# One encoder layer on one core: w_down's squares moved into the joint MLP, and five smaller changes of order, banks and queues

## The chip, the cores and the metric

The kernel runs on one core of a Trainium2 chip as one launch. The metric is device time in microseconds (us), from the start of the program to its end. The engines are TensorE (PE), VectorE (DVE), ScalarE (ACT), GpSimd (POOL) and SyncE (SP). SP, ACT and POOL also issue DMA transfers, each in its own order; all transfers of the core run on the same 16 DMA engines.

## The reference

One layer of an encoder on 2048 tokens of width 1024, in float32, cut here to what is computed:

```python
y = rmsnorm(h, norm_mix_g) @ w_in                    # q, k, v (8 heads of 64) and the conv's a, g
att = dilated_sliding_attention(q, k, v)             # three patterns (window, stride), joined by their lse
conv = silu(layernorm(depthwise_conv31(a * sigmoid(g))))
h = h + concat(att, conv) @ w_out
xq = rmsnorm(h, norm_x_g) @ w_xq                     # 4 heads of 256 against 256 memory tokens
h = h + softmax(xq @ xk.T) @ xv @ w_xo               # xk, xv = rmsnorm(mem) @ w_xk, w_xv
u = rmsnorm(h, norm_mlp_g) @ w_up                    # 1024 -> 4096
h = h + square(relu(u)) @ w_down                     # 4096 -> 1024
out = rmsnorm(h, norm_final_g)
```

## The kernel before, in words

**Arithmetic.** A float32 operand is split into a high part (a cast, mostly on ACT) and a low part (operand minus high part, mostly on DVE), and a product is three matmuls: high by high, low by high, high by low (`mm3`, L270 to L272). So every weight block of 128x1024 is loaded, cast (`whi_…`), subtracted (`wlo_…`) and then used by PE. Where the parts are float16, the weights are first scaled by a power of two that comes from the sum of the weight's squares (`pow2_scale`), so that the low parts do not vanish.

**Stages.** The 2048 tokens are four quarters p = 0 to 3 of 512.

1. 0 to about 390 us: `w_in`. The norm and transposes of x for each quarter (`xprep`: `xn`, `xv`, `xh`, `xl`), the products `lin` with the weight blocks `g0` … `a3` of the conv (`lwhi_g20` is the high part of block g2's weights, L226), q, k, v, RoPE. A generator `steps` walks PE's products; others are woven into it. `later` is the x work of quarters 2 and 3, `qks` the squares of the q and k weights (ACT L781, loads on SP). ACT's Sigmoid (`sig`, L672) empties the PSUM bank of a `lin`.
2. About 390 to 690 us: attention of quarter 0, with the memory's products beside it (class `Matrices`). `load(i)` fetches weight block i (0 to 15 w_xk and w_xv, 16 to 23 w_xq, 24 to 31 w_xo) on POOL's queue, into a ring of two buffers `raw` that w_out's blocks `raw_o…` use next, or, for 26 to 29, into buffers of their own in the pool `back_w`, which opens when the attention's pool closes. `turn` transposes w_xq (PE writes bank `xqt`, ACT copies the high part, DVE subtracts the low part, L539 to L542), `score` multiplies it by the memory's keys, `back` multiplies w_xo by the memory's values (`pb`) and stores the result (`eb` to `bscr`) on POOL's queue. `ps(tag, …)` takes a PSUM bank: "mm" has two, "T" two more, which the attention's transposes use.
3. About 690 to 1310 us, `post(0)`, and to 1860 us, `post(1)`: w_out (`o`), cross attention (`xs`, `x`) and the MLP (`up`, `dn`) of a quarter, with the attention of the next quarter beside it. In `post(0)` each MLP block's low part is stored to DRAM (`lou`, `lod`), and `post(1)` loads it back. In `post(1)` ACT also squares every block of w_up and w_down, 32 each, and sums the squares (`wsq`, L1571), for the scales of stage 5.
4. To about 2145 us: `before_mlp(2)` and `(3)`, the same without the MLP.
5. From about 2137 us: the MLP of quarters 2 and 3 together, as a 2x2 block product with seven products in place of eight (Strassen's scheme: `b11`, `b21`, `t1` … are sums of quarters of the operands). In the first half, 7 early products (`PRO`, weights `whi_ua0` … `whi_ua6`, result `r11_…`) precede 16 calls of `up_pair`; DVE forms sums of the bank's results (`r`), ACT applies Relu (L1812) and Square (L1813, which also sums), and POOL's queue stores the result (`keep_r`, `rb`, `rt`). In the second half four sweeps p, q, r, s over the 16 pairs multiply by w_down; each step loads a hidden block and its weights, scales and splits them (`bh`, `bl`, `whi`, `wlo`, L1798 and L1799) and runs 12 matmuls for each of its one or two products. Between the sweeps DVE adds the seven products into the result: `plus` (L1986, SBUF with SBUF) and `join` (L1989, with a bank).

Each engine runs its instructions in the order that a scheduler fixed when the program was built; `after(…)`, `pinned` and `weave` only steer that order. An attention pattern's result `o1` goes to DRAM (`oscr`) and is loaded again by `combine` (`ld`), since it has another token order.

## Time and profile before

| | |
|---|---|
| median of 3 runs | 2778.16 us (2777.91 to 2783.6) |
| the profiled execution | 2774.07 us, span 2772.3 us |
| PE busy | 2661.1 us of the span, 96% |
| DVE, ACT, POOL busy | 1918.8, 1359.5, 589.4 us |
| DMA | 535.68 MB, mean 193 GB/s |

The profile is of one execution. Its own time stands 1.8 us above its span, and 4.1 us below the median. PE's 14,787 matmuls are pipelined, so a busy PE is not one at its peak: in some stretches its clock is granted only half, and a matmul of 512 columns then starts every 0.43 us instead of every 0.216 us. Such stretches count as busy; the column PEclk of the windows shows them.

### The profile page before, as it was taken

To read this page: it belongs to the slowest core of one execution; us is meant where nothing else is said; L and a number is where in the kernel's file an instruction comes from. 1 tells how busy PE (TensorE), PEld (TensorE's weight loads), DVE (VectorE), ACT (ScalarE), POOL (GpSimd) and SP (SyncE) were. 2 spreads that over 40 slices of the span, in tenths; PEclk is the share of its full clock that TensorE was granted. 3 is DMA by queue.
4 is the path that set the end of the run, shared out by engine and by line. 5 is a ranking of instruction groups with operands and counts; after the bars stand their busy time and mean duration, and the time that the engine had idled before them with its cause. 6 is when DMAs were issued, how large, how long until landed. Compare 5 with 4: busy or idle time off the path is not lost.

```text
span 2772.3 us, 40744 instructions
## 1 busy us (share of the span) xinstructions
PE 2661.1 (96%) x14787; PEld 1831.0 (66%) x14787; DVE 1918.8 (69%) x3508; ACT 1359.5 (49%) x2354; POOL 589.4 (21%) x807
## 2 busy tenths in 40 slices
PE   7899999988999999999999999999999999989998
PEld 4444457876777878788777777877887444434444
DVE  4568726665788876578976477756475887767776
ACT  6742217655454333434455555564343545545445
POOL 6474313543102212200111201121010122200000
PEclk9999999999999999999999999999999999999999
DMA  7874457887636666766457766764633564485553
GB/s 252 217 200 113 135 182 200 244 238 229 200 114 204 203 220 208 246 215 208 133 177 225 240 210 201 238 226 158 190 114 126 178 205 167 168 304 170 171 189 110
DMA packets 459816, 535.68 MB, mean 193 GB/s; under 512 B 98172, under 2 KB 329200, under 8 KB 459616
## 3 DMA queue, kind: packets, MB, share of 16 engines
q1 hardware_dynamic: 420992, 406.52, 48.5%
q0 software_dynamic: 36752, 123.06, 12.7%
q10 hardware_dynamic: 1872, 3.52, 0.3%
q8 instruction: 116, 1.90, 0.3%
q14 instruction: 84, 0.69, 0.1%
HBM read 384.46 MB, written 148.52 MB: 192 GB/s over the span
## 4 chain that ended last, share of the span: by engine, by line
PE 60%; DMA 13%; issue 11%; ACT 5%; DVE 5%; POOL 4%; SPq 2%; POOLq 0%; ACTq 0%; DVEq 0%
PE dn L270 4%; PE dn L271 4%; PE dn L272 4%; PE up L270 3%; PE up L272 3%; PE up L271 3%; PE lin L270 2%; PE lin L272 2%; PE lin L271 2%; SPq L57 2%; PE x L270 2%; PE x L271 2%; PE x L272 2%; PE xs L270 2%; PE xs L272 2%
## 5 line engine op out<-in xcount | busy, mean ns | idle before, releaser
L287 DVE SCALAR_TENSOR_TENSOR cacc<-cu,cwu,cacc 128x512 f32<-128x512 f32 x480 | 395.6, 826 | 6.8
L1032 ACT ACTIVATE sm<-sm,o 128x256 f32<-128x256 f32 (+1 forms) x384 | 159.2, 466 | 115.3 <-DVE o L1031 114.8
L270 PE MATMUL dn<-hhh,whi_d 128*128 128x512 f32 x512 | 202.1, 405 | 5.8 <-ACT hhh L1591 3.5
L270 PE MATMUL up<-mh,whi_u 128*128 128x512 f32 x512 | 203.9, 399 | 1.7 <-ACT whi_u L1567 1.7
L271 PE MATMUL dn<-hhl,whi_d 128*128 128x512 f32 x512 | 200.6, 394 | 0.8 <-DVE hhl L1592 0.8
L272 PE MATMUL up<-mh,wlo_u 128*128 128x512 f32 x512 | 200.0, 391 | 0.0
L272 PE MATMUL dn<-hhh,wlo_d 128*128 128x512 f32 x512 | 199.9, 393 | 0.0
L271 PE MATMUL up<-ml,whi_u 128*128 128x512 f32 x512 | 199.6, 390 | 0.0
L1042 DVE TENSOR_TENSOR pl<-pt,ph 128x512 f16<-128x512 f32 x160 | 109.6, 685 | 80.3 <-ACT ph L1041 79.8
L1031 DVE CUSTOM_DVE_ANT_0 sm<-s,mask 128x256 f32<-128x256 f32 (+1 forms) x384 | 126.6, 373 | 33.5 <-DMA oscr<-o 11.8
L1041 ACT CAST ph<-pt 128x512 f16<-128x512 f32 x160 | 92.2, 576 | 77.0 <-PE pt L1038 76.3
L1606 DVE TENSOR_TENSOR h<-h,dn 128x512 f32<-128x512 f32 x128 | 85.9, 682 | 55.6 <-PE dn L272 55.0
L247 POOL TENSOR_TENSOR nr<-st_v,mhalf 128x4 f32<-128x4 f32 x12 | 13.2, 1098 | 513.2 <-DVE st_v L243 513.2
L270 PEld LDWEIGHTS dn<-hhh,whi_d 128*128 128x128 f32 x512 | 95.5, 188 | 25.8 <-ACT hhh L1591 5.2
L272 PEld LDWEIGHTS dn<-hhh,wlo_d 128*128 128x128 f32 x512 | 96.6, 189 | 20.3
L270 PEld LDWEIGHTS up<-mh,whi_u 128*128 128x128 f32 x512 | 96.2, 188 | 20.6 <-ACT whi_u L1567 2.0
L271 PEld LDWEIGHTS dn<-hhl,whi_d 128*128 128x128 f32 x512 | 96.7, 189 | 19.6 <-DVE hhl L1592 1.8
L272 PEld LDWEIGHTS up<-mh,wlo_u 128*128 128x128 f32 x512 | 96.1, 188 | 20.5
L271 PEld LDWEIGHTS up<-ml,whi_u 128*128 128x128 f32 x512 | 96.3, 188 | 18.6
L270 PE MATMUL o<-cath,whi_o 128*128 128x512 f32 x256 | 103.0, 403 | 4.3 <-ACT whi_o L261 3.6
L272 PE MATMUL o<-cath,wlo_o 128*128 128x512 f32 x256 | 101.5, 398 | 1.4 <-DVE wlo_o L262 1.4
L1038 PE MATMUL pt<-ident,sm 128*128 128x128 f32 x640 | 100.1, 274 | 2.7 <-ACT sm L1032 2.5
(647 smaller groups left out, 7835.8 us busy)
## 6 DMA issues: line engine op xcount, KB each, us to landing
raw_u<-in_w_up_dram SPq DMA_DIRECT2D x64, 512.0 KB
raw_d<-in_w_down_dram SPq DMA_DIRECT2D x64, 512.0 KB
k<-kscr SPq DMA_DIRECT2D x32, 640.0 KB
raw_a<-ascr SPq DMA_DIRECT2D x32, 512.0 KB
raw_b<-bscr SPq DMA_DIRECT2D x32, 512.0 KB
lou<-wlo_u POOLq DMA_DIRECT2D x32, 512.0 KB, 5.4
lod<-wlo_d POOLq DMA_DIRECT2D x32, 512.0 KB, 5.5
wlo_u<-lou SPq DMA_DIRECT2D x32, 512.0 KB
```

Source lines behind the costliest of these rows:

```text
L57: return (q or nc.sync).dma_start(o, i)
L247: last["pow"] = POOL.tensor_tensor(dst, v, mhalf.to_broadcast([P, v.shape[1]]), op=ALU.pow)
L270: PE.matmul(o, lh, rh, start=first, stop=False)
L271: PE.matmul(o, lh, rl, start=False, stop=False)
L272: last["pe"] = PE.matmul(o, ll, rh, start=False, stop=end)
L287: DVE.scalar_tensor_tensor(acc, u[:, t:t + 512], cwu[:, c, t:t + 1], acc, op0=ALU.mult, op1=ALU.add)
L1031: last["dve"] = DVE.tensor_tensor_reduce(dst, so, mask[:, 256 * m:256 * m + nk], 1.0, 3e38, ALU.add, ALU.min, mn)
L1032: last["act"] = ACT.activation(dst, dst, AF.Exp, bias=mn, scale=-1.0)
L1038: last["pe"] = PE.transpose(pt[:, j, :], sm[:, j, :], ident)
L1041: ACT.copy(ph, pt)
L1042: DVE.tensor_tensor(pl, pt, ph, op=ALU.subtract)
L1606: last["dve"] = DVE.tensor_tensor(hs[m], hs[m], pt, op=ALU.add)
```

## The change

Seven edits, in the order of the program.

**(a)** `last["g2"]` is set where `steps` reaches the cast of block g2, and `later` and `qks` may be placed only behind it.

**(b)** `turn`'s second transpose bank (g = 1) comes from "T" instead of "mm": four banks in turn instead of two.

**(c)** Blocks 26 and 27 of w_xo now use the ring `raw`, and 28 to 31 the buffers of `back_w`; 26 and 27 are loaded as soon as the ring is free, and `raw_o00` and `raw_o01` find it free earlier.

**(d)** 13 stores `oscr<-o1` move from ACT's queue to POOL's.

**(e)** In `post(1)` the squares of w_down go; those of w_up stay.

**(f)** In the first half of stage 5 a new generator `down_squares` loads w_down once more, 32 loads of 512 KB on POOL's queue into two buffers in turn, and ACT squares each in place with a sum. Three steps of it follow each of the first two pairs, and two each of the next. Then a sum over the 32 columns, one small matmul and `pow2_scale` give the scale that the sweeps use. Some small columns change their tile (`cw` and `wscl` swap roles).

**(g)** 4 of DVE's `plus` go from behind sweep q into sweep q, and 12 from ahead of sweep r's joins and sweep s into sweep r, one per step from the third step on.

```diff
@@ class Matrices
-            if 25 < i < 30:
+            if i > 27:
                 raw = self.bl.tile([P, 2, 512], F32, tag=f"rb{i}", name=f"raw_m{i}")
...
-                    pt = ps("mm", f"xqt{i}{g}")
+                    pt = ps("T" if g else "mm", f"xqt{i}{g}")
...
-            if i < 26:
-                self.load(i + 6)
...
                 if mc == 0:
                     self.split(i + 1)
+                    if i == 24:
+                        self.load(27)
@@ w_in
         drain(islice(steps, 10))
+        last["g2"] = last["split"]
...
-        later = pinned(chain(xprep(sp, 2), islice(mem, 1), xprep(sp, 3), mem), "x1_7", "flo", "pe")
-        qks = pinned(qkscale(), "x1_7", "xs1")
+        later = pinned(chain(xprep(sp, 2), islice(mem, 1), xprep(sp, 3), mem), "x1_7", "g2", "flo", "pe")
+        qks = pinned(qkscale(), "x1_7", "g2", "xs1")
@@ attention
-                    os_.rearrange("p b h e -> p b (h e)"), None if far and pr < 3 else nc.scalar)
+                    os_.rearrange("p b h e -> p b (h e)"), None if far and pr < 3 else nc.gpsimd)
...
             mats.split(24)
+            mats.load(26)
...
-            for i in range(26, 30):
+            for i in range(28, 32):
                 mats.load(i)
@@ def wmlp (post(1))
-        j = tmp("wsq").bitcast(BF16).rearrange("p (a b) -> p a b", a=shape[1])
-        x = i + (DFF // P if w == "d" else 0)
-        ACT.activation(j, raw, AF.Square, accum_out=fw[:, x:x + 1])
+        if w == "u":
+            j = tmp("wsq").bitcast(BF16).rearrange("p (a b) -> p a b", a=shape[1])
+            ACT.activation(j, raw, AF.Square, accum_out=fu[:, i:i + 1])
@@ joint MLP, first half
+    def down_squares():
+        sq = [pm.tile([P, D], F32, tag="dsq", name=f"dsq{k}", bufs=2) for k in range(2)]
+        for k in range(DFF // P):
+            if k > 1:
+                sq[k % 2] = pm.tile([P, D], F32, tag="dsq", name=f"dsq{k}", bufs=2)
+            dma(sq[k % 2], w_down[P * k:P * k + P], nc.gpsimd)
+            yield
+            if k:
+                t = sq[(k - 1) % 2]
+                ACT.activation(t, t, AF.Square, accum_out=wscl[:, k - 1:k])
...
+        DVE.tensor_reduce(v[:, 0:1], wscl, axis=AX.X, op=ALU.add)
+        norm_scale("d", c30, v, mc[:, 1:2], mc[:, 3:4])
+        yield
...
     for i in range(NP):
         prev = up_pair(i, early_pairs[i] if i < PRO else None, prev)
+        drain(islice(down, 3 if i < 2 else 2))
+    drain(down)
     prev()
@@ sweeps
-    def sweep(tag, blocks, weights, kinds):
+    def sweep(tag, blocks, weights, kinds, side=iter(())):
...
+            if k > 1:
+                next(side, None)
+        drain(side)
...
-    m4, m6 = sweep("q", ("t4", "t2"), w_second, "XY")
+    m4, m6 = sweep("q", ("t4", "t2"), w_second, "XY", adds([(HD_[2][m], e1[m]) for m in range(4)]))
     for m in range(4):
-        plus(HD_[2][m], e1[m], DVE)
...
-    m2, m5 = sweep("r", ("b21", "t1"), w_third, "XY")
+    m2, m5 = sweep("r", ("b21", "t1"), w_third, "XY",
+                   adds([x for m in range(4) for x in ((HD_[2][4 + m], e7[m]), (HD_[3][4 + m], e7[m]),
+                                                       (HD_[3][m], e1[m]))]))
...
-    for m in range(4):
-        plus(HD_[2][4 + m], e7[m], DVE)
-        plus(HD_[3][4 + m], e7[m], DVE)
-        plus(HD_[3][m], e1[m], DVE)
```

What this moves in the fixed orders is shown at three places. First ACT near 66 us of the span, before the change. `xn2`, `xn3` are x's rows of quarters 2 and 3, `qks` loaded weights of q and k, `sig0_1` the Sigmoid that empties the bank in which PE's next product starts:

```order
L381 ACTIVATE junk_940,ssx2_933<-xn2_1_1_916 128x512
L781 ACTIVATE qks00_960,qka_959<-qks00_960 128x512
L381 ACTIVATE junk_942,ssx2_933<-xn2_2_0_919 128x512
L781 ACTIVATE qks01_963,qka_959<-qks01_963 128x512
L381 ACTIVATE junk_944,ssx2_933<-xn2_2_1_920 128x512
L381 ACTIVATE junk_946,ssx2_933<-xn2_3_0_923 128x512
L381 ACTIVATE junk_948,ssx2_933<-xn2_3_1_924 128x512
L381 ACTIVATE junk_1276,ssx3_1275<-xn3_0_0_1211 128x512
L226 CAST lwhi_g20_693<-lraw_g20_679 128x1024
L672 ACTIVATE sig0_1_988<-lin_899,wscl_328 128x512
```

The same place on ACT with the change:

```order
L419 CAST xh3_1_416<-xv1_7_866 128x512
L226 CAST lwhi_g20_693<-lraw_g20_679 128x1024
L381 ACTIVATE junk_934,ssx2_933<-xn2_0_0_911 128x512
L781 ACTIVATE qks00_960,qka_959<-qks00_960 128x512
L781 ACTIVATE qks01_963,qka_959<-qks01_963 128x512
L672 ACTIVATE sig0_1_988<-lin_899,wscl_328 128x512
```

The cast of g2's weights now leads, and one x square and two q/k squares stand ahead of the Sigmoid instead of eleven such squares, of which eight are shown, and the cast.

Second, POOL's queue near 660 us, before the change (`eb` are results of `back` on their way to `bscr`; `raw_m30` and `raw_m31` were issued some 20 rows earlier, and `raw_o00` follows seven `bscr` stores later):

```order
L57 DMA bscr_111<-eb000_7811 128x4x128
L57 DMA bscr_111<-eb010_7821 128x4x128
L57 DMA raw_m26_7772<-in_w_xo_dram 128x2x512
L57 DMA raw_m27_7774<-in_w_xo_dram 128x2x512
L57 DMA raw_m28_7776<-in_w_xo_dram 128x2x512
L57 DMA raw_m29_7778<-in_w_xo_dram 128x2x512
L57 DMA bscr_111<-eb001_7847 128x4x128
L57 DMA bscr_111<-eb011_7857 128x4x128
```

The same place on POOL with the change (`raw_m26` and `raw_m27` have taken the earlier places of 30 and 31):

```order
L57 DMA bscr_111<-eb000_7813 128x4x128
L57 DMA bscr_111<-eb010_7823 128x4x128
L57 DMA raw_m28_7774<-in_w_xo_dram 128x2x512
L57 DMA raw_m29_7776<-in_w_xo_dram 128x2x512
L57 DMA raw_m30_7778<-in_w_xo_dram 128x2x512
L57 DMA raw_m31_7780<-in_w_xo_dram 128x2x512
L57 DMA raw_o00_8093<-in_w_out_dram 128x8x128
L57 DMA bscr_111<-eb001_7847 128x4x128
L57 DMA bscr_111<-eb011_7857 128x4x128
L57 DMA raw_o01_8099<-in_w_out_dram 128x8x128
```

The four loads at this place are now of blocks that PE needs two blocks later, and w_out's first two loads stand here.

Third, ACT near 2146 us, in the early products, before the change (`r11_0` from `b1_0` is the Relu that empties the bank in which PE's next early product starts, the second `r11_0` its Square, `whi_ua5` the next weights, `Y…` casts of operands):

```order
L1812 ACTIVATE r11_0_22181<-b1_0_22153,wscl_328 128x512
L1826 COPY c1_1_22204<-b1_1_22191 128x512
L1547 COPY rsb3_20571<-nrb_21997 128x512
L1813 ACTIVATE r11_0_22181,cw_322<-r11_0_22181 128x512
L1724 CAST Yb22h0_22025<-yn3_01_22037 128x512
L1724 CAST Yt1h0_22048<-yt1_0_22042 128x512
L1724 CAST Yt2h0_22009<-yt2_0_22043 128x512
L1724 CAST Yt3h0_22017<-yt3_0_22052 128x512
L1798 ACTIVATE whi_ua5_22339<-raw_ua5_22337,wscl_328 128x1024
L1812 ACTIVATE r11_1_22219<-b1_1_22191,wscl_328 128x512
```

The same place on ACT with the change:

```order
L1817 ACTIVATE r11_0_22117<-b1_0_22089,cw_322 128x512
L1831 COPY c1_1_22140<-b1_1_22127 128x512
L1549 COPY rsb3_20507<-nrb_21933 128x512
L1907 ACTIVATE dsq1_22441,wscl_328<-dsq1_22441 128x1024
L1818 ACTIVATE r11_0_22117,cw_322<-r11_0_22117 128x512
L1729 CAST Yb22h0_21961<-yn3_01_21973 128x512
L1729 CAST Yt1h0_21984<-yt1_0_21978 128x512
L1729 CAST Yt2h0_21945<-yt2_0_21979 128x512
L1907 ACTIVATE dsq2_22445,wscl_328<-dsq2_22445 128x1024
L1729 CAST Yt3h0_21953<-yt3_0_21988 128x512
L1803 ACTIVATE whi_ua5_22275<-raw_ua5_22273,cw_322 128x1024
L1817 ACTIVATE r11_1_22155<-b1_1_22127,cw_322 128x512
```

Two squares of w_down stand between one Relu and the next, and the second waits for a load that may start only when the square two before it is done. On ACT, 16 of the 32 squares stand ahead of the last early Relu, `r11_6`, and all 32 ahead of `r4_2`, the first result of the fifth pair.

More of the change, by code (lines that the diff above doesn't have):

```diff
@@ L1662, in hybrid_layer, with norm_scale @@
     late = ExitStack()
+    def norm_scale(x, c30, v, c, inv):
+        pc = ps("c", f"fwp{x}")
+        with ExitStack() as st:
+            after(st, "pe")
+            PE.matmul(pc[:, 0:1], c30, v[:, 0:1], start=True, stop=True)
+        DVE.tensor_scalar(v[:, 2:3], pc[:, 0:1], 1e-30, None, op0=ALU.max)
+        pow2_scale(c, inv, v[:, 2:3], v[:, 4:5], -1)
     def mlp_scales():
@@ L1668, in mlp_scales @@
         DVE.memset(c30, 2.0 ** -30)
-        DVE.tensor_reduce(v[:, 0:2], fw.rearrange("p (x k) -> p x k", x=2), axis=AX.X, op=ALU.add)
+        DVE.tensor_reduce(v[:, 0:1], fu, axis=AX.X, op=ALU.add)
         g8 = gv[:, GV["mlp"]:GV["mlp"] + 8]
@@ L1673, in mlp_scales @@
         yield
[L1674 to L1679 removed]
+        norm_scale("u", c30, v, mc[:, 0:1], mc[:, 2:3])
         yield
@@ L1690, in mlp_scales @@
         yield
-    mc, gml = wscl[:, 0:16], wscl[:, 16:24]
+    mc, gml = spare[:, 96:112], spare[:, 112:120]
     scales = mlp_scales()
@@ L1891, in up_pair @@
         return rest
+    def down_squares():
[8 more added lines that the diff above has]
+                ACT.activation(t, t, AF.Square, accum_out=wscl[:, k - 1:k])
+        t = sq[(DFF // P - 1) % 2]
+        ACT.activation(t, t, AF.Square, accum_out=wscl[:, 31:32])
+        yield
+        v = spare[:, 64:80]
+        c30 = pm.tile([P, P], F32, name="c30d")
+        DVE.memset(c30, 2.0 ** -30)
+        DVE.tensor_reduce(v[:, 0:1], wscl, axis=AX.X, op=ALU.add)
+        norm_scale("d", c30, v, mc[:, 1:2], mc[:, 3:4])
+        yield
+    down = down_squares()
     early_pairs = [True] * PRO
@@ L1998, in hybrid_layer, with adds @@
             dma(HD_[p][k], hscr[p, k])
-    m4, m6 = sweep("q", ("t4", "t2"), w_second, "XY")
+    def adds(items):
+        for a, b in items:
+            plus(a, b, DVE)
+            yield
+    m4, m6 = sweep("q", ("t4", "t2"), w_second, "XY", adds([(HD_[2][m], e1[m]) for m in range(4)]))
     for m in range(4):
-        plus(HD_[2][m], e1[m], DVE)
         join(HD_[2][4 + m], m4[m], HD_[2][4 + m])
```

8 lines of the change are left out of this document (1 added, 7 removed).

## The prediction

> **What bounds the kernel now.** First the page's list of engines, then PE's waits.
>
> ```profile
> PE 2661.1 (96%) x14787; PEld 1831.0 (66%) x14787; DVE 1918.8 (69%) x3508; ACT 1359.5 (49%) x2354; POOL 589.4 (21%) x807
> ```
>
> PE is the bound: it idles 2772.3 - 2661.1 = 111 us. No edit takes matmuls away (one tiny one is added), so only this idle time and the time at half clock can be won. PE's waits, as total, times and longest:
>
> ```profile
> PE r L271 <- DVE bl_r L1799: 6.9, 3, 3.8
> ...
> PE xqt L539 <- DVE wlo_m L542: 6.1, 5, 1.8
> PE lin L270 <- ACT sig L672: 6.1, 1, 6.1
> ...
> PE b L1791 <- ACT r L1812: 5.2, 4, 1.6
> ...
> PE pb L270 <- ACT whi_m L261: 3.9, 1, 3.9
> ...
> PE o L270 <- ACT whi_o L261: 3.6, 2, 3.3
> ...
> PE dn L270 <- ACT hhh L1591: 3.5, 6, 1.1
> ...
> PE dn L270 <- ACT whi_d L1567: 2.3, 3, 1.3
> ...
> PE pb L271 <- DVE wlo_m L262: 0.8, 1, 0.8
> ```
>
> Each of these but `b` is aimed at by one edit; `b` is the one that (f) may lengthen. A wait costs more than itself where the clock drops behind it, which the windows show (PE busy is the first column, the clock the number behind the counts, then DMA share and GB/s):
>
> ```profile
> 70.00:78.00 8.00, 1.89 (x12) 1.16 (x11) 2.49 (x9) 6.52 (x17) 1.83 (x2) 0.81 0.46 163
> 78.00:85.00 7.00, 6.36 (x17) 2.51 (x16) 4.11 (x9) 7.00 (x18) 3.28 (x3) 0.50 0.90 268
> 664.00:672.00 8.00, 3.37 (x10) 2.43 (x9) 3.17 (x4) 2.74 (x4) 2.16 (x3) 0.80 0.96 305
> 690.00:700.00 10.00, 6.36 (x17) 4.04 (x16) 6.67 (x21) 2.48 (x4) 2.21 (x3) 0.66 1.03 360
> 1714.00:1726.00 12.00, 10.30 (x53) 7.20 (x52) 6.98 (x11) 10.44 (x19) 0.00 (x0) 0.86 0.60 187
> 2140.00:2180.00 40.00, 34.22 (x162) 15.70 (x160) 33.69 (x54) 26.24 (x48) 7.15 (x12) 1.00 0.42 135
> 2627.00:2647.00 20.00, 14.40 (x59) 6.04 (x58) 20.00 (x29) 9.52 (x14) 0.00 (x0) 0.91 0.50 150
> ```
>
> Half of what PE works at half clock is lost. From 78 to 85 us that is 6.36 / 2, with a little before it 3.5 us. A mean of 0.80 over 8 us is 3.2 us at half clock, nearly all worked, so 1.5 us lost; 0.66 over 10 us is 6.8, so 3.2; 0.86 over 12 us is 3.4, so 1.6; 0.91 over 20 us is 3.6, so 1.7.
>
> **The change part by part.**
>
> (a) The cast of g2. ACT around it now:
>
> ```profile
> 71.38 0.63 ACT L781 ACTIVATE qks<-qks 128x512 f32<-128x512 f32 x1 [5.49 <-DMA qks<-in_w_in_dram]
> ...
> 76.11 1.03 ACT L226 CAST lwhi_g<-lraw_g 128x1024 f16<-128x1024 f32 x1
> 77.04 0.68 ACT L672 ACTIVATE sig<-lin,wscl 128x512 f32<-128x512 f32 x1
> ```
>
> PE waits for the Sigmoid. In the new order two q/k squares still stand ahead of it, and the first has its data only at 71.4, so the Sigmoid ends near 71.4 + 2 x 0.8 + 0.7 = 73.7: 4.1 of the 6.1 us go. A wait of 2 us is no longer than those of `xqt`, so the 3.5 us of clock go too, by my estimate. But the next weights, g3, are now cast behind two more q/k squares, whose loads SP issues only after others at a DMA share of 0.9, while PE comes 4 us earlier: I take 3 us back. Gain 5, between 0 and 9.6.
>
> (b) Four banks. With two more, a transpose waits for the subtraction four groups back, not two. The attention uses these banks as well, so I take 4 of 6.1, between 0 and 6.1.
>
> (c) w_xo and w_out. From 640 to 720 us, KB each and median to landing:
>
> ```profile
> raw_o<-in_w_out_dram POOLq DMA_DIRECT2D x6, 512.0 KB, 7.0
> raw_m<-in_w_xo_dram POOLq DMA_DIRECT2D x4, 512.0 KB, 7.2
> ```
>
> Blocks 26 and 27 are now loaded before the attention's buffers come free, so 3.9 + 0.8 and 1.5 of clock go. Block 28 inherits the late place, but PE needs it some 7 us after block 26 (24 matmuls of 0.23 us and some of the attention's), against the 3.9 by which block 26 came late: I leave 1 us, since the four loads at this place slow one another, gain 5. Block o00 is asked for ahead of seven stores: 3.3 us of wait and 3.2 of clock may go; but 690 to 700 us has a DMA share of 1.03, the same bytes must arrive, and PE comes 6 us earlier. The stores that the two loads pass are read only in `post(0)`. I take 4. Gain 9 in all, between 3 and 6.2 + 3.6 + 3.2 = 13.
>
> (d) The stores on POOL. ACT loses 13 issues; POOL's in-order queue gains them, and `oscr3_1` now sits behind the `bscr` store of `eb111`. The combine that reads it ends on DVE, and PE transposes its result:
>
> ```profile
> 697.44 1.41 DVE L1170 TENSOR_TENSOR cat<-cat,ld 128x512 f32<-128x512 f32 x2
> ...
> 709.89 0.60 PE L1178 MATMUL catT<-ident,cat 128*128 128x128 f32 x4
> ```
>
> That leaves 11 us of slack, which (c) shortens by about 4. 0, between -2 and +2.
>
> (e) No squares of w_down in `post(1)`.
>
> ```profile
> L1571 ACT ACTIVATE wsq<-raw_d 128x1024 bf16<-128x1024 f32 x32 | 33.6, 1049 | 0.0
> ```
>
> ACT gives up 33.6 us, but it was not the bound; the worth is PE's waits for it: 3.5 for `hhh` (queued behind a square), 2.3 for `whi_d` (its load starts when the square has let the buffer go), 1.6 of clock. What is late next is the DMA of the same blocks. 5, between 2 and 7.4.
>
> (g) The sums. DVE between sweeps q and r:
>
> ```profile
> 2629.43 1.89 DVE L1986 TENSOR_TENSOR hd<-hd,e 128x512 f32<-128x512 f32 x3
> 2631.24 1.27 DVE L1799 SCALAR_TENSOR_TENSOR bl_r<-braw_r,wscl,bh_r 128x1024 f16<-128x1024 f32 x1
> 2632.43 5.50 DVE L1986 TENSOR_TENSOR hd<-hd,e 128x512 f32<-128x512 f32 x9
> ...
> 2640.38 1.27 DVE L1799 SCALAR_TENSOR_TENSOR bl_r<-braw_r,wscl,bh_r 128x1024 f16<-128x1024 f32 x1
> 2641.58 0.74 DVE L1799 SCALAR_TENSOR_TENSOR wlo_r<-raw_dd,wscl,whi_r 128x512 f16<-128x512 f32 x1
> ...
> 2646.62 0.68 DVE L1982 TENSOR_TENSOR keep<-raw_dd,keep 128x512 f32<-128x512 f32 x1
> ```
>
> Twelve sums of 0.61 us stood ahead of the `bl_r` that PE waited for (6.9 us, and 1.7 of clock). One a step, they fit: a step costs DVE two `wlo_r`, one `bl_r` and two of the last kind, 4.1 us, and PE works 24 x 0.216 = 5.2. The joins stay, so I take 5 of 8.6, at least 2.
>
> (f) The squares in the joint MLP: the one cost. ACT in the early products now:
>
> ```profile
> 2146.54 0.67 ACT L1812 ACTIVATE r<-b,wscl 128x512 f32<-128x512 f32 x1
> ...
> 2152.43 1.15 ACT L1798 ACTIVATE whi_ua<-raw_ua,wscl 128x1024 f16<-128x1024 f32 x1 [0.22 <-PE b L1791]
> 2153.48 0.67 ACT L1812 ACTIVATE r<-b,wscl 128x512 f32<-128x512 f32 x1
> ...
> 2188.40 0.67 ACT L1812 ACTIVATE r<-b,wscl 128x512 f32<-128x512 f32 x1
> ```
>
> The first two and the last (`r11_6`) of the early Relus: a pair takes 6.9 us, and PE already waits for the Relu in four of them (5.2 in all), so ACT's chain sets the pace here, although ACT is busy only 26 of 40 us. Sixteen squares at 1.05 us stand ahead of the last early Relu: 16.8 us. ACT idles 1 to 2.5 us in a pair, some 10 over six, so at least about 7 us remain on the path. Behind each square also its load's landing waits, with the weights and Relus of the next pair queued behind it. No row shows these loads; the nearest of 512 KB on POOL's queue:
>
> ```profile
> lou<-wlo_u POOLq DMA_DIRECT2D x32, 512.0 KB, 5.4
> ```
>
> and in (c) 7.2 where the DMA share was 1. From 2140 to 2262 us POOL's queue tells what they add:
>
> ```profile
> q0 software_dynamic: 3200, 10.49, 22.1%
> ```
>
> 10.49 MB took 22.1% of 122 us, 2.6 us of all engines a MB; 32 loads are 16.8 MB, 43 us within the 116 us (2146 to 2262) in which the new order has them. That adds 0.37 to the share of 0.42 that the windows show, about 0.8, so I take 6 us for a landing. Two buffers make a round of two squares cost landing, square and issue, 6 + 1.05 + 0.5 = 7.6 us; the fourteen squares behind the first two take seven rounds, 53 us, where the early Relus now span 42: 11 us later. At 5.4 it is 49 and so 7, ACT's own bound; at 7.2, 61 and 19. The other sixteen have 74 us for eight rounds of 61: hidden. The scale of w_down is now known only at the end of the first half, where ACT and DVE wait anyway; 1 us for that. Cost 12, between 4 (ACT absorbs more than I count) and 35 (below).
>
> The Trainium skill, "DMA: Bandwidth & Descriptors", section "Anatomy of one DMA — SWDGE (gpsimd) path", gives a DMA from GpSimd as about 2.0 us plus its bytes at 436 GB/s, 3.2 us for 512 KB (an estimate from that page). The trace's 5.4 and 7.2 disagree; by the page the loads would never be last and (f) would cost 8 in place of 12.
>
> **Sum.** 5 + 4 + 9 + 0 + 5 + 5 = 28, less 12: 16 us. The profiled execution's 2774.07 would become 2758; that execution lies 4.1 under the median, so I forecast 2762 us.
>
> **The rivals.**
>
> *The waits come back.* The loads of g3, the combine, or the same DMA that is full at 660 to 700 us end last next, and of the 28 only 14 stay: 14 - 12 = 2 us, 2776. For it: shares of 0.9 to 1.03 at (a) and (c). Against: (e) and (g) wait for no full DMA. This is also the case in which the change does not do what it says.
>
> *All of it holds and the squares hide.* Upper ends 9.6 + 6.1 + 13 + 7.4 + 8.6 = 45, less 4 to 8: 2737 to 2741. For it: 14 us of ACT's 40 are idle there. Against: PE's `b` row.
>
> *The squares drop the clock: slower.* If a landing takes 7.2 us, the early products last 19 us longer, 3 us of PE idle in each pair. Above about 3 us of idle the clock fell (3.9 and 3.3 above), and it did at 1714 us with 1.7 us of idle in all. PE's 34 us of work at half clock cost up to 17 more: 36 against 28, 2786 with the median's 4. It decides where (f) exceeds 28, at landings near 7 us with the clock down in more than half the pairs. Against it: pairs with 1.6 us of idle kept 1.00.
>
> The Trainium skill, "TensorE: Matmul & The Clock Gate", section "HAM oscillation — how this bites in real kernels", names idle gaps over about 3.4 us as what drops the clock. The 0.86 at 1714 us disagrees; by the page this rival needs landings above 7.2 and its chance would be halved.
>
> **How the numbers follow.** The forecast, by its terms' inner bounds 2750 to 2772, gets 0.60; waits that come back 0.16; all holds 0.12; the clock 0.12. About 5.5 us (0.2%) is what a measurement of this kernel can tell from none. Faster by more: 0.60 + 0.12 and a small part of the second, 0.75; within 0.2%: 0.13; slower by more: 0.12. The range for 8 in 10 takes in the first rival whole and the near end of the second: 2740 to 2782, which leaves out the third from its decision point up and the far end of the second.
>
> **What would show it.** (a) `lin` from `sig` near 2 us and the clock whole at 78 to 85; a new wait for `lwhi_g` is the price. (b) `xqt` under 2 us. (c) No `pb` from `whi_m` of 3.9, and `o` from `whi_o` under 1. (e) `dn` from `hhh` and `whi_d` under 2 together. (g) `r` from `bl_r` under 2. (f) `b` from `r` L1812 at 15 or more, ACT's square rows with idle from its DMA, landings of 5.4 to 7. Wrong would be landings near 4, or a clock under 1.00 at 2140 to 2200.

## The result, and the profile after

| | before | after |
|---|---|---|
| median of the runs (4 each) | 2778.03 us (2773.46 to 2783.6) | 2821.22 us (2818.06 to 2825.32) |
| the profiled execution | 2774.07 us, span 2772.3 | 2825.32 us, span 2823.3 |

The change makes the kernel slower: ratio 1.0155, 95% interval 1.0131 to 1.0179, some 43 us by the medians and 51 by the two profiled executions. The forecast was 2762 us, 16 faster. From the page of the changed kernel:

```profile
PE 2673.8 (95%) x14789; PEld 1834.9 (65%) x14789; DVE 1922.7 (68%) x3514; ACT 1358.9 (48%) x2354; POOL 611.7 (22%) x852
```

PE idles 2823.3 - 2673.8 = 149.5 us where it idled 111, and is busy 12.7 us longer with two tiny matmuls more, which fits the lower clock shown below. To see where, take the start of the n-th matmul on a tile in both traces and subtract (worked out from the two traces, us):

| place | after less before | stretch | adds |
|---|---|---|---|
| first matmul on `pxk`, end of `w_in` | +13.5 | (a) | 13.5 |
| first matmul on `o` (w_out, quarter 0) | +16.0 | attention, (b), (c) | 2.5 |
| 60th on `o` | +23.7 | (c), (d) | 7.7 |
| 577th on `o` (first of quarter 3), behind `post(1)` | +23.7 | (e) | 0 |
| 60th on `b`, early products | +24.7 | | 1 |
| 180th on `b` | +35.4 | early products, (f) | 10.7 |
| last on `b` | +52.1 | pairs, (f) | 16.7 |
| end | +51.0 | sweeps, (g) | -1.1 |

PE's waits in the changed kernel (total, times, longest), against those the prediction quotes:

```profile
PE opt L1049 <- DVE pl L1043: 14.7, 7, 6.7
PE lin L270 <- DVE rope_kr L874: 10.8, 2, 6.1
PE b L1796 <- ACT r L1817: 9.2, 4, 3.1
PE o L272 <- DVE wlo_o L262: 9.2, 2, 8.7
PE b L1796 <- DVE r L1866: 8.0, 1, 8.0
PE r L271 <- DVE bl_r L1804: 7.0, 4, 3.8
PE b L1796 <- DVE r L1875: 6.6, 9, 1.5
...
PE lin L270 <- DVE stl_k L887: 5.0, 1, 5.0
...
PE dn L270 <- ACT hhh L1593: 4.6, 5, 1.3
...
PE lin L270 <- ACT sig L672: 1.5, 1, 1.5
```

The waits that (a), (b) and (c) aimed at are gone: `sig` fell from 6.1 to 1.5, `xqt` and `pb` from `whi_m` no longer appear. In their places stand longer ones that were short or not there: `rope_kr`, `opt`, `wlo_o`. `bl_r` is as it was (7.0 for 6.9). The windows of the changed kernel (PE busy first; clock, DMA share and GB/s last):

```profile
64.00:100.00 36.00, 34.14 (x169) 16.62 (x167) 8.70 (x31) 27.20 (x69) 9.12 (x6) 1.00 0.90 233
150.00:180.00 30.00, 17.91 (x74) 8.20 (x72) 10.71 (x16) 14.30 (x22) 15.80 (x21) 0.77 0.78 215
2160.00:2220.00 60.00, 46.81 (x201) 20.56 (x200) 43.30 (x67) 45.20 (x84) 15.83 (x28) 0.91 0.72 234
2250.00:2274.00 24.00, 13.27 (x55) 5.31 (x54) 13.90 (x19) 10.52 (x19) 7.27 (x14) 0.86 0.78 265
2676.00:2696.00 20.00, 14.40 (x61) 6.13 (x60) 20.00 (x30) 9.36 (x13) 0.00 (x0) 0.94 0.40 130
```

The aimed-at place of (a) is whole: clock 1.00 from 64 to 100 us. But from 150 to 180 PE now works 17.9 of 30 us at 0.77. The same 30 us before:

```profile
150.00:180.00 30.00, 30.00 (x143) 13.91 (x142) 16.68 (x16) 16.13 (x22) 23.38 (x18) 1.00 0.89 235
```

ACT at that place, changed kernel; in brackets the idle time ahead and what ended it:

```profile
170.80 1.15 ACT L225 ACTIVATE lraw_q<-lraw_q,qkc 128x1024 f32<-128x1024 f32 x1 [7.67 <-DMA lraw_q<-in_w_in_dram]
171.96 0.58 ACT L872 COPY sw_kr<-lin 64x512 f32<-64x512 f32 x1
```

The same scaling before:

```profile
171.15 1.15 ACT L225 ACTIVATE lraw_q<-lraw_q,qkc 128x1024 f32<-128x1024 f32 x1 [0.17 <-DMA lraw_q<-in_w_in_dram]
```

The weights come at the same time in both, 171 us. PE, ahead of its old schedule here (by 8 us at the 433rd matmul on `lin`), runs into them: ACT waits 7.67 us in order for a weight block that is not needed yet, and the copies `sw_kr` that empty the bank of PE's present product are queued behind it. The lead is handed back with interest: the 529th matmul on `lin` starts 10 us late, and the clock falls too.

The second such place is `post(0)`. DVE in the changed kernel:

```profile
720.58 0.17 DVE L1143 TENSOR_TENSOR csm<-ld 128x8 f32<-128x8 f32 x1 [10.70 <-DMA ld<-oscr]
720.78 0.17 DVE L1144 TENSOR_TENSOR csm<-csm,o 128x8 f32<-128x8 f32 x1
720.87 1.22 DVE L262 TENSOR_TENSOR wlo_o<-raw_o,whi_o 128x1024 fp32r<-128x1024 f32 x1
```

DVE stands 10.70 us before a combine whose data is still in flight, with the low half of w_out's next block, which PE needs, right behind it.

The third is (f). SP's queue, ACT and DVE in one pair, changed kernel, one fence for each:

```profile
2253.62 0.44 SPq L57 DMA_DIRECT2D raw_ub<-in_w_up_dram  x1
```

```profile
2257.69 1.06 ACT L1907 ACTIVATE dsq<-dsq 128x1024 f32<-128x1024 f32 x1 [0.64 <-DMA dsq<-in_w_down_dram]
...
2267.00 0.72 ACT L1803 ACTIVATE whi_uu<-raw_ub,cw 128x512 f16<-128x512 f32 x1 [8.16 <-DMA raw_ub<-in_w_up_dram]
```

```profile
2267.07 0.69 DVE L1849 TENSOR_TENSOR s<-raw_ub 128x512 f32<-128x512 f32 x1 [8.10 <-DMA raw_ub<-in_w_up_dram]
```

`raw_ub` is issued at 2253.62 and there at 2267.0, 13.4 us later (in the kernel before, where an engine waits for it, it takes 4.8 to 7.0 us from issue to first use), and both engines wait 8 us for it; PE then waits 8.0 for `r` L1866, which stands behind it on DVE.

### The profile page after: what moved, and what is told of

Read it like the earlier page. It is cut to its first block, busy times and chain, and to the rows that moved or that the text cites. A ratio compares the mean times of both kernels' runs of the same rounds, so it can differ in the third digit from the quotient of the medians.

```text
span 2823.3 us, 40836 instructions
## 1 busy us (share of the span) xinstructions
PE 2673.8 (95%) x14789; PEld 1834.9 (65%) x14789; DVE 1922.7 (68%) x3514; ACT 1358.9 (48%) x2354; POOL 611.7 (22%) x852
## 5 line engine op out<-in xcount | busy, mean ns | idle before, releaser
L1032 DVE CUSTOM_DVE_ANT_0 sm<-s,mask 128x256 f32<-128x256 f32 (+1 forms) x384 | 126.7, 373 | 39.8 <-DMA oscr<-o 15.5
```

Source lines behind the costliest of these rows:

```text
L1032: last["dve"] = DVE.tensor_tensor_reduce(dst, so, mask[:, 256 * m:256 * m + nk], 1.0, 3e38, ALU.add, ALU.min, mn)
```

## The experiments

Theory 1 is the reading above: the losses are places where an engine meets, in its fixed order, data that land late, and each edit makes its own. Its rivals changed with the runs. The kernel before was run beside each group of kernels; its medians there were 2772.0 to 2774.0 us. Times "over before" below are differences of the medians within a group; each ratio stands with its 95% interval. What is read from a trace is of one execution, and the executions of one kernel lie up to some 15 us apart. The expectations also call a quarter of the tokens a text group, the first to the fourth, and `post(1)`'s MLP the dense MLP of the second.

### Each edit by itself

`a_alone` has edit (a), `b_alone` edit (b), `c_alone` edit (c), `ef_alone` edits (e) and (f), each as in the change:

```diff
+        last["g2"] = last["split"]                        # a_alone, with both pins below
-                    pt = ps("mm", f"xqt{i}{g}")           # b_alone
+                    pt = ps("T" if g else "mm", f"xqt{i}{g}")
-            if 25 < i < 30:                               # c_alone
+            if i > 27:
+    down = down_squares()                                 # ef_alone
```

> The kernel before with edit (a) alone. Theory 1 (each edit has a cost of its own): PE's start on g2 comes 4 to 5 us earlier, but ACT then waits in order for the weights lraw_q1, which land near 171 us whatever PE does, with the copies that empty PE's banks queued behind; PE's waits for rope_kr and stl_k come to about 15 us and the kernel is 13 us slower, near 2791. Rival (the stall needs the other edits): 5 us faster, near 2773, with no rope_kr wait over 2 us.

2784.56 us, ratio 1.0047 [1.0033, 1.0061]: 12 us slower, with `lin` from `rope_kr` at 10.9 and from `stl_k` at 4.9, as in the whole change. The loss is (a)'s own.

> The kernel before with edit (b) alone. Theory 1: xqt's waits go (6 us), but the combine's load of an attention pattern, which stands at a fixed place in DVE's order, is not there yet when PE comes earlier; DVE waits for ld for 9 us, PE for pl, and the kernel is 2 to 6 us slower. Rival: the ld wait in the changed kernel came from the delay that edit (a) put ahead of it; then (b) alone is 4 us faster.

2772.27 us, ratio 1.0004 [0.999, 1.0019]: nothing, between the two. The waits of `xqt` are gone, but PE waits elsewhere, and DVE (second fence, from 500 to 600 us) shows for what:

```profile
PE opt L1048 <- DVE pl L1042: 10.2, 7, 5.7
```

```profile
DVE csm L1142 <- DMA ld<-oscr: 9.1, 1, 9.1
```

PE comes up to 6.4 us earlier and meets a combine whose data are there at nearly the time they were before (565 us, 567 before): DVE waits 9.1 us for them where it waited 4.3, with `pl` behind.

> The kernel before with edit (c) alone (the attention's last store stays on ACT's queue). Theory 1: pb's wait of 3.9 us and its clock go, 7 us, but the DMA that is full at 660 to 700 us ends last: DVE waits 10 us for ld with wlo_o behind it, and 7 of 7 us come back: within 2 us of before. Rival: that wait of DVE came from edit (d), which put the store that ld reads on POOL's queue behind the stores of w_xo's results; then (c) alone is 6 to 9 us faster.

2776.09 us, ratio 1.0012 [0.9996, 1.0028]: not told from nothing. Neither the wait for `ld` that Theory 1 named nor the rival's gain is there. The wait for `whi_m` has gone into this one:

```profile
PE pb L270 <- ACT eb L583: 14.6, 2, 12.9
```

> The kernel before with edits (e) and (f), which need one another. Theory 1: the squares' loads cost 11 us in the early products and 15 more behind them, where raw_ub comes late, and (e) wins 0 to 4 us in post(1): 24 to 28 us slower, near 2804. Rival (half of this is the phase in which the earlier edits left the loads): 10 to 14 us slower.

2806.17 us, ratio 1.0119 [1.0096, 1.0143]: 33 slower (27 to 40 by the interval), rather more than was expected of Theory 1. This is most of the change's loss.

> Only edit (d), the attention's pattern stores on GpSimd's queue. The prediction: within 2 us of before. Rival, a store that lands later delays the combine that loads it back: 3 to 8 us slower.

2769.73 us, ratio 0.9992 [0.9981, 1.0003]: nothing that can be told, as predicted, though its median lies 3.7 us lower.

```diff
-                    ... None if far and pr < 3 else nc.scalar)
+                    ... None if far and pr < 3 else nc.gpsimd)
```

> Edits (c) and (d) together. If the late load of the second combine in the changed kernel comes of the two together: 5 to 11 us slower than before, more than c_alone and d_alone make. If not: their sum, some 3 us.

Edits (c) and (d): 2769.83 us, ratio 0.9987 [0.9977, 0.9996], 3.6 us faster; as d_alone's median lies 3.7 below too, what (c) adds to that is not shown. The wait of c_alone is nearly gone:

```profile
PE pb L270 <- ACT eb L583: 2.3, 2, 1.7
```

In c_alone ACT stood idle until its own store `oscr` had gone out at 681.62 us, with PE's `pb` behind it; (d) takes this store off ACT:

```profile
682.00 1.04 ACT L261 CAST whi_m<-raw_m 128x1024 fp32r<-128x1024 f32 x1 [13.55 <-DMA catl<-catl]
```

But the wait of the changed kernel is here in cd_both, on DVE and with it on PE, whose next operand `qh` is late as well:

```profile
696.32 0.17 DVE L1142 TENSOR_TENSOR csm<-ld 128x8 f32<-128x8 f32 x1 [10.67 <-DMA ld<-oscr]
```

```profile
PE s L1231 <- DMA qh<-qscr: 10.4, 1, 10.4
```

So the 10.70 us before the combine in the changed kernel go with (c) and (d) together: they are 10.67 here, and at this place 4.07 in d_alone, none in c_alone, and 2.5 to 7.0 in the kernels with neither. The load of `ld` is issued when the store of `oscr` has landed, and from that store's issue to the combine it is 22.3 us here and 21.2 in the changed kernel, against 12.8 in d_alone and 12.1 before (worked out from the traces). PE starts on `o` 10.8 us ahead of before and is 1.0 ahead at the 60th matmul: this stretch takes the lead back, and so the late load does not show as a loss against before. In the changed kernel, which comes to this place 16 us late, the same stretch adds 7.7. Which transfers delay the store and the load, those that (c) puts there or others, was not tried.

By the medians the parts run so far make 12 - 1 - 4 + 33 = 40 of the whole's 43 us. With their intervals that leaves room for some 10 us either way, and by the traces the parts do not simply add: the stretch of w_out loses 7.7 us in the whole, and (f)'s stretches cost 26 us there and 32 in ef_alone (the table below).

### Which half of (a)

```diff
-        later = pinned(..., "x1_7", "g2", "flo", "pe")     # a_qks
+        later = pinned(..., "x1_7", "flo", "pe")
-        qks = pinned(qkscale(), "x1_7", "g2", "xs1")       # a_later
+        qks = pinned(qkscale(), "x1_7", "xs1")
```

> Only the squares of w_q and w_k are held behind the cast (half of edit (a)); the preparation of the third and fourth text groups stays where it was. Theory L (the moved preparation and its stores hold up the next weight loads): 5 us faster to 2 us slower than before. Theory Q (the moved squares make the scale, or the loads behind them, late): 8 to 14 us slower.

2775.47 us, ratio 1.0004 [0.9989, 1.0019]: nothing that can be told.

> Only the preparation of the third and fourth text groups is held behind the cast; the squares of w_q and w_k stay where they were. Theory L: 8 to 14 us slower than before, with the wait of the q rotation in the page. Theory Q: within 3 us of before.

2785.66 us, ratio 1.0041 [1.0026, 1.0056], 12 slower. Its ACT at the same instruction:

```profile
166.46 1.15 ACT L225 ACTIVATE lraw_q<-lraw_q,qkc 128x1024 f32<-128x1024 f32 x1 [5.38 <-DMA lraw_q<-in_w_in_dram]
```

Theory L holds as to the half that costs: the moved preparation of quarters 2 and 3, not the moved squares. Its mechanism is not seen: the weights themselves do not come later than before (166 us for 171). PE came earlier by more: its 433rd matmul on `lin` started 10.2 us ahead of before and its 529th 7.1 us behind. How much of that swing of 17 us is the wait, the copies behind it and the clock was not separated.

### (e) without (f), and (f) taken apart

In `e_only` the squares of w_down stand nowhere and the sum is a constant, so w_down's scale is left out. `f_loads` has the 32 loads without squares, `f_squares` the 32 squares on a resident tile without loads; in these too the sum is not w_down's.

```diff
     def down_squares():
+        DVE.memset(wscl[:, 0:32], 1.0)                                    # e_only: only this
-            dma(sq[k % 2], w_down[P * k:P * k + P], nc.gpsimd)            # f_squares: without the load
-                ACT.activation(t, t, AF.Square, accum_out=wscl[:, k - 1:k])   # f_loads: without this
```

> w_down's squares are taken out of the second text group's dense MLP and stand nowhere: no loads, no squares in the joint MLP, and the sum of squares is a constant (the scale of w_down is so left out). What (e) is worth by itself. By the prediction's term 5 us less than before (2 to 7.4 us). The rival, that the matrix products there wait for something else in turn: within 2 us of before.

2770.33 us, ratio 0.9998 [0.9986, 1.001]: (e) is worth nothing that can be told. PE's waits in `post(1)` are what they were (3.5 and 2.3 before):

```profile
PE dn L270 <- ACT hhh L1591: 4.7, 5, 1.7
...
PE dn L270 <- ACT whi_d L1567: 1.7, 2, 1.1
```

> Edits (e) and (f) with the 32 loads of w_down in the joint MLP's first half, but without their squares (left out; the sum is a constant), so ScalarE has no more to do than in e_only. Theory 1, the transfers delay what the matrix products wait for: 18 to 30 us more than e_only. Theory 2, ScalarE's 32 squares and its waits for the loads, ahead of its other work, are the cost: at most 6 us more than e_only. The prediction's own sum: 6 to 11 us more.

2785.53 us, ratio 1.0042 [1.0025, 1.006].

> Edits (e) and (f) with the 32 squares on a tile that is there already, and no loads (w_down's values are left out of the sum). Theory 1 (transfers): at most 5 us more than e_only. Theory 2 (ScalarE's time): 15 us or more above e_only.

2788.8 us, ratio 1.0055 [1.0038, 1.0071]. Against e_only the loads cost 15 us and the squares 18: neither Theory 1 nor Theory 2 alone. That they make 34 of the 35 by which ef_alone lies above e_only is no split of it, since without loads to wait for the squares stand elsewhere: 27 of them ahead of the 180th matmul on `b` in f_squares, 13 in ef_alone. Loads and squares stood early: the scheduler lifts whatever has its data. GpSimd's order in the changed kernel, from the first early product on, shows it (an excerpt of the program, not of a trace):

```
L57 DMA dsq_22440<-in_w_down_dram 128x1024
L57 DMA dsq_22441<-in_w_down_dram 128x1024
L247 TENSOR_TENSOR nr<-st_v,mhalf 128x4
L57 DMA c1s_22076<-c_0_22102 128x512
L57 DMA dsq_22445<-in_w_down_dram 128x1024
L57 DMA c1s_22077<-c_1_22140 128x512
L57 DMA dsq_22564<-in_w_down_dram 128x1024
```

The code asks for three steps after the first pair; the loads stand ahead of the first early product's store.

### Other places for the same loads and squares

To hold a load at a place, it is put behind a store `keep_r` on its own queue:

```diff
+                after(st, "kr")
                 dma(sq[k % 2], w_down[P * k:P * k + P], nc.gpsimd)
-        drain(islice(down, 3 if i < 2 else 2))
+        drain(islice(down, 0 if i < 7 else 4))      # ef_late; ef_mid: 0 if i < 3 else 3; ef_fit: 0 if i < 7 else 5
```

> Edits (e) and (f) whole, with the same 32 loads and squares, but each load is held behind a store of the pair before and none is issued before the eighth pair: the DMA engines are busy 0.38 to 0.53 there before the change, where they are 0.47 to 0.68 in the stretch into which the scheduler lifted the loads. Theory 1, narrowed to that stretch (a DMA system near its limit): at most 10 us more than before, a fall of 20 us or more against ef_alone's +33. Rival: 32 loads and squares cost 25 to 33 us wherever they stand in the first half.

2795.06 us, ratio 1.0081 [1.0066, 1.0096], 23 slower: neither the one number nor the other.

> Edits (e) and (f) whole; the loads are held as in ef_late, but start at the fourth pair, three to a pair, so that the last ends some two pairs before the half does. Theory 1 (the price lies in the stretch before the pairs and in the last load's tail, not in loads and squares as such): within 5 us of before. Rival, a price of some 1 us for each load and its square in the pairs: 15 us or more slower than before.

2792.79 us, ratio 1.0075 [1.005, 1.01], 19 slower. Theory 1 as it stood there is refuted.

> Edits (e) and (f) whole; loads held as in ef_late, but five to a pair from the eighth pair to the fourteenth, so that they neither meet the spilled products of the first seven pairs nor end after the half's last matrix products. Theory 1 (two places in the half that are short of time, and room between them): within 6 us of before, where ef_mid (from the fourth pair) and ef_late (to the end) were 19 and 22 us slower. Rival, a price for each load and square wherever they stand: 15 us or more slower than before.

2797.78 us, ratio 1.0092 [1.0079, 1.0106], 24 slower. With this the theory of two short places has fallen: the same loads and squares cost 19 to 33 us at each of the four places tried. When, is told by the start of the n-th matmul on `b` against before, counted from the 60th (worked out from the traces, one execution each, us):

| | 180th | 420th | 780th | 1020th | 1140th | last | end |
|---|---|---|---|---|---|---|---|
| after | 10.7 | 25.3 | 26.3 | 26.0 | 27.2 | 27.3 | 26.3 |
| e_only | 0 | -1.0 | -2.8 | -3.1 | -2.6 | -2.6 | -3.1 |
| ef_alone | 5.7 | 25.6 | 28.4 | 28.0 | 32.3 | 32.5 | 32.3 |
| f_loads | 4.2 | 11.3 | 8.7 | 8.5 | 9.2 | 9.8 | 8.4 |
| f_squares | 9.3 | 9.8 | 10.4 | 10.1 | 10.9 | 11.1 | 10.5 |
| ef_mid (from pair 4) | 0 | 0.1 | 15.3 | 16.2 | 17.6 | 19.3 | 16.9 |
| ef_late (from pair 8, to the end) | 0 | 0 | -1.2 | 0.2 | 4.4 | 20.0 | 21.8 |
| ef_fit (pairs 8 to 14) | 0 | 0.1 | -1.4 | 1.6 | 10.1 | 20.5 | 19.3 |
| ef_fit_rub (below) | -0.6 | -0.7 | -4.3 | -4.6 | -4.1 | 3.7 | 10.6 |
| ef_rub (below) | 8.5 | 19.0 | 15.7 | 15.4 | 15.4 | 15.5 | 14.3 |
| fit_squares (below) | 0 | 0.2 | -0.1 | 1.1 | 1.1 | 4.2 | 2.8 |

The loss sets in where the loads and their squares do. e_only, which has neither, shows that differences of some 3 us mean little here. In ef_late a part is another thing, the tail: the scale's small matmul stands in PE's order and waits for the last square.

```profile
2454.39 0.59 PE L1668 MATMUL fwpd<-cw,c30d 128*128 128x1 f32 x2 [6.85 <-DVE cw L1914]
```

### What the loads hold up

In ef_fit, PE idles behind DVE and ACT, and these wait for this (2160 to 2440 us):

```profile
DVE s L1847 <- DMA raw_ub<-in_w_up_dram: 30.6, 10, 6.5
...
ACT whi_uu L1801 <- DMA raw_ub<-in_w_up_dram: 20.9, 6, 4.8
```

The same window of before; the wait was there already, 3.2 at the longest on DVE, and PE had the room for it:

```profile
DVE s L1844 <- DMA raw_ub<-in_w_up_dram: 30.1, 14, 3.2
...
ACT whi_uu L1798 <- DMA raw_ub<-in_w_up_dram: 16.9, 5, 5.1
```

It is the loads rather than the squares that make `raw_ub` late: from issue to first use, where an engine waits for it, it takes 4.8 to 7.0 us before, up to 7.9 in f_squares and fit_squares, but up to 12.2 in f_loads, 13.8 in ef_alone and 10.8 in ef_fit (worked out from the traces).

`raw_um` and `raw_ub` take turns in two buffers, so each of a pair's loads can start only when the pair before has read that buffer. Two kernels give `raw_ub` two buffers of its own, and one takes the loads away at ef_fit's places (w_down's values are left out of its sum):

```diff
-        rb_ = wraw(wcols(w_up, (i + 16) * P), f"ub{i}")                               # ef_fit_rub, ef_rub
+        rb_ = pm.tile([P, 8, P], F32, tag="rub", name=f"raw_ub{i}", bufs=2)
+        dma(rb_, wcols(w_up, (i + 16) * P))
-                dma(sq[k % 2], w_down[P * k:P * k + P], nc.gpsimd)                    # fit_squares
+                POOL.memset(sq[k % 2][:, 0:1], 1.0)
```

> ef_fit with two buffers of its own for raw_ub, which has taken turns with raw_um in two buffers, so that a pair's second weight load can start a pair earlier. Theory R (the added loads make raw_ub late, and nothing but it): at most 8 us slower than before, where ef_fit was 24. Theory S (ScalarE's squares and its waits for their loads, ahead of the splits that the matrix products need): 16 us or more slower.

2783.6 us, ratio 1.0032 [1.002, 1.0044]: 10.5 slower where ef_fit was 24. Theory R's bound of 8 lies within the interval (5.5 to 12.2), Theory S's 16 outside it. The waits for `raw_ub` in the same window are one line:

```profile
ACT whi_uu L1801 <- DMA raw_ub<-in_w_up_dram: 1.8, 1, 1.8
```

The 1140th matmul on `b`, 10.1 us late in ef_fit, is 4.1 early here, with the loads and squares where ef_fit has them, and more bytes a second: the first line is ef_fit's window, the second this kernel's.

```profile
2300.00:2450.00 150.00, 133.63 (x594) 57.97 (x593) 91.48 (x127) 101.51 (x188) 44.12 (x82) 0.97 0.73 247
```

```profile
2300.00:2450.00 150.00, 139.90 (x628) 61.41 (x626) 98.38 (x141) 107.09 (x200) 47.82 (x89) 0.97 0.77 262
```

What remains comes at the end of the half (from 4.1 early to 3.7 late at the last matmul on `b`) and in the sweeps (10.6 at the end); of these 7 us some 4 lie at sweep r, where the wait for `bl_r` is 9.5 us here and differs from kernel to kernel with no edit there (5.2 in ef_mid, 9.3 in e_only).

Not all of the 14 us need be the loads': the buffers were not given to the kernel before. At the 780th matmul, which only the first of the loads precede, this kernel is 4.3 early and ef_fit 1.4.

> Edits (e) and (f) as in the change, with the two buffers of raw_ub as in ef_fit_rub. Theory R: at most 18 us slower than before, where ef_alone was 33 (the 10 to 12 us of the early products stay, which use no raw_ub). Theory S: 28 us or more slower.

2792.88 us, ratio 1.0065 [1.0052, 1.0078]: 20 slower where ef_alone was 33, 2 over Theory R's bound and 8 under Theory S's. 8.5 of it is there at the 180th matmul, in the early products, which have no `raw_ub`; another 10.5 still comes in the first pairs, to the 420th, where ef_alone lost 19.8.

> ef_fit's squares at ef_fit's places, on resident tiles, without the loads (w_down's values are left out of the sum). Theory R: within 6 us of before. Theory S: 12 us or more slower.

2776.83 us, ratio 1.0017 [1.0006, 1.0028]: 4 slower, Theory R. 32 squares cost little in the pairs; 27 of them ahead of the 180th matmul cost 9 (f_squares above).

### The sums, really moved

Edit (g) alone leaves on each engine the same instructions in the same order as before, so there is no run of it; in the traces too DVE's order from sweep q to the end of r is the same in the changed kernel as before, but for one instruction that moves by one place. `g_pin` holds each sum behind the low halves of its step:

```diff
             scaled(bh, bl, braw, cr)
+            last["bl"] = last["sc"]                       # DVE's last instruction in scaled
-    ... adds([...]))
+    ... pinned(adds([...]), "bl"))
```

> Edit (g) with each sum held on VectorE behind the low halves of its step's blocks, so that the order of VectorE really changes (edit (g) by itself gives the same instructions in the same order as before). If the prediction's step (g) was right and only the order failed: 2 to 6 us less than before. Rival, the matrix products between the sweeps wait for something else in turn, or for the sums in the steps: within 2 us of before or slower.

2763.26 us, ratio 0.9965 [0.995, 0.998]: some 10 us faster than before (6 to 14 by the interval), and the fastest kernel here. By the traces 8.5 of it lie between the first matmul on `q` and the last on `r`. PE's wait, 6.9 us in three before and 5.2 to 9.5 in all other kernels here:

```profile
PE r L271 <- DVE bl_r L1799: 1.3, 1, 1.3
```

```profile
2627.00:2647.00 20.00, 18.74 (x86) 8.30 (x85) 17.74 (x24) 12.98 (x17) 0.00 (x0) 1.00 0.82 269
```

PE works 18.74 of these 20 us at clock 1.00, where it worked 14.40 at 0.91. DVE now takes one sum a step:

```profile
2633.68 1.28 DVE L1799 SCALAR_TENSOR_TENSOR bl_r<-braw_r,wscl,bh_r 128x1024 f16<-128x1024 f32 x1
2634.88 0.68 DVE L1990 TENSOR_TENSOR hd<-hd,e 128x512 f32<-128x512 f32 x1
...
2637.41 1.27 DVE L1799 SCALAR_TENSOR_TENSOR bl_r<-braw_r,wscl,bh_r 128x1024 f16<-128x1024 f32 x1
2638.60 0.68 DVE L1990 TENSOR_TENSOR hd<-hd,e 128x512 f32<-128x512 f32 x1
```

In the changed kernel the sums stand where they stood, in a row, with nine of them ahead of the next `bl_r`:

```profile
2680.18 1.89 DVE L2017 TENSOR_TENSOR hd<-hd,e 128x512 f32<-128x512 f32 x3
2681.98 1.27 DVE L1804 SCALAR_TENSOR_TENSOR bl_r<-braw_r,cw,bh_r 128x1024 f16<-128x1024 f32 x1
2683.18 5.49 DVE L2017 TENSOR_TENSOR hd<-hd,e 128x512 f32<-128x512 f32 x9
```

## Why the prediction was wrong, step by step

| step | predicted | measured by itself | |
|---|---|---|---|
| (a) | gain 5 | loss 12 (a_alone) | the price was mis-sized |
| (b) | gain 4 | 0 | the wait went elsewhere |
| (c), (d) | gain 9 and 0 | gain 4 (cd_both; d_alone 4 too, not told from 0) | PE 11 us ahead at `o`, handed back at the combine's load |
| (e) | gain 5 | 2, not told from 0 | the squares were not what those waits hung on |
| (g) | gain 5 | 0 as edited, 10 as meant | the order did not change |
| (f) | loss 12 | loss 35 (ef_alone less e_only) | the pairs' share, put at nothing |

**(f)** is the largest, and the step that failed is the term that was put at nothing: "The other sixteen have 74 us for eight rounds of 61: hidden." It asked only whether the loads and squares find room for themselves. It did not ask what the loads do to the load that the pairs wait for. The waits for `raw_ub` stood in the trace of before (30.1 us on DVE, 16.9 on ACT), and the added loads lengthen what `raw_ub` takes, from 7.0 us at most to as much as 13.8. The pairs, with the end of the half, cost 16.7 where 0 and 1 were put; for the end alone the 1 is about right (1.3 between the 1020th and the last matmul).

The early products, the part that was worked out, came out as said, 11 us predicted and 10.7 measured, but in part by luck. The landings of `dsq` were 5.4 us (5.1 in the early products) where 6 was taken, and by the prediction's own sum 5.4 makes 7, not 11. The clock, 0.91 from 2160 to 2220 us, is a term that the 11 did not have: some 11 us at half clock, of which half at most is lost (an estimate from that row). How the 10.7 divides was not separated.

**(a)** The prediction had the right wait and the right end of it (2 us predicted, 1.5 measured, clock 1.00), and it named a price at the next weights, "while PE comes 4 us earlier". The price was some 17 us, and came 90 us later, at a load that (a) did not touch: a late load costs its own wait, that of the copies behind it on ACT, and the clock. **(b)** and **(c)** met what the first rival had named, waits that come back: at a combine's load near 565 us, and at `eb` or, with (d), at the combine's load ahead of w_out. That rival (2776) was right on mechanism and had left the signs of (e), (f) and (g) to the forecast.

**(g)** "One a step, they fit" was right: g_pin gains the whole 8.6 that was set as the most (8.5 by the traces). What failed is that nothing looked whether the edit moved anything on DVE. The case in which "the change does not do what it says" was put in one with the waits that come back and never held against this edit.

**The slow rival.** It had the sign, by the wrong mechanism: landings were 5.4, not 7.2, and the clock took only a part. Its price for the clock was also half of what its own condition gives: the 34 us of PE's work were measured at clock 1.00, so at half clock they take 34 us more, not 17. But the clock did fall at short gaps. In the early products of the changed kernel PE's longest idle time was 3.1 us:

```profile
2170.00:2180.00 10.00, 5.34 (x24) 2.34 (x24) 8.32 (x13) 9.17 (x18) 2.73 (x5) 1.00 0.67 215
2180.00:2190.00 10.00, 7.23 (x25) 2.87 (x25) 9.94 (x16) 9.10 (x18) 2.72 (x5) 0.83 0.84 265
```

0.83 behind gaps of 2.25 and 3.05 us, which ended at 2172.0 and 2180.4. The Trainium skill, "TensorE: Matmul & The Clock Gate", section "HAM oscillation — how this bites in real kernels", gives idle gaps above about 3.4 us as the abstract rule, and beside it tells of a kernel whose frequent short idle times did it. This trace agrees with the second and not with the first, as 1714 us did before.

**The prediction's own signs.** Those of (a), (b) and (c) came. Those of (e), (f) and (g) did not: `hhh` alone was 4.6, `b` from `r` L1817 was 9.2 where 15 was named, with 8.0 and 6.6 at other `r` instead, and `bl_r` was 7.0. A clock under 1.00 at 2140 to 2200, which was named as a sign of being wrong, was there.

**What stays open.** Why the rest of (f) is as large as it is: with `raw_ub`'s own buffers 8.5 us in the early products and 10.5 in the first pairs of ef_rub, and 7 in the sweeps of ef_fit_rub; loads and squares were not separated there. Whether `raw_ub` suffers from the bytes of the added loads or from the order in which the DMA engines serve the queues was not tried. Which transfers make the combine's load late with (c) and (d) is open, and so is how much of the 13 to 14 us that the buffers gave they would have given the kernel before.

## What to carry to other kernels

Ahead of moving transfers into a stretch, look in its trace for the loads that engines already wait for without harm to the bound; they are what the new transfers will make late, and room of its own for such a load went with 13 to 14 us less here, as much as the best choice of place. Removing a wait early in the program moves PE forward onto loads that come when they always came; price the next late load, not only the wait that goes. An edit of the source is not an edit of the order: compare what each engine executes in sequence, before counting its gain.

## What was not expected of the hardware

27 squares of 1.05 us on ACT cost 9 us to the 180th matmul, among early products whose pace ACT's chain sets (f_squares); 32 of them among the pairs cost 1 us to the 1140th matmul and 4 to the last on `b` (fit_squares). The landings of `dsq` kept a median of 5.2 to 5.4 us in the changed kernel, ef_alone, ef_fit and ef_fit_rub alike; what the crowding lengthened was another queue's load, `raw_ub`, issued on SP, which took 13.4 us at 2253 us in the changed kernel and at most 7.0 before, where an engine waited for it.
